# A two-layer hybrid encoder trunk on one core: the token sublayer resequenced, and eight of 22 up tiles as seven half-size products

## The chip, the cores and the metric

The kernel runs on one core of a Trainium2 chip, written by hand in a tile framework: the program names tiles and engines, the framework adds the semaphores and, where the program does not fix an order, plans the order of each engine's instructions by its own costs. The engines are PE (TensorE, matmuls and transposes), DVE (VectorE), ACT (ScalarE), POOL (GpSimd) and SP (SyncE, which only issues DMAs here). POOL issues DMAs too, among them all that add to what lies in the destination. The metric is the device time of one execution in microseconds (us).

## The reference

Two layers on x of 512 tokens by 1024 channels, all float32. Each layer has a token sublayer (attention over a 2-D neighbourhood with 8 heads, bidirectional retention with 4 heads, two sigmoid gates, an output projection, LayerNorm) and a channel sublayer (a gated MLP with a depthwise convolution over three tokens, a gated per-layer embedding, LayerNorm).

```python
for i in range(DEPTH):
    proj = x @ w_in[i]
    q_na, k_na, v_na, q_r, k_r, v_r, g_r, gate_a, gate_b = jnp.split(proj, IN_SPLITS, axis=-1)
    ya = neighbourhood_attention(q_na, k_na, v_na, na_rpb[i])      # heads of 64
    yb = bidirectional_retention(q_r, k_r, v_r, g_r, ret_decay_f[i], ret_decay_b[i])
    merged = jax.nn.sigmoid(gate_a) * (ya @ w_branch_a[i]) + jax.nn.sigmoid(gate_b) * (yb @ w_branch_b[i])
    y = merged @ w_out[i]
    x = layer_norm(DEEPNORM_ALPHA * x + y, ln1_g[i], ln1_b[i])
    ffn = conv_glu_ffn(x, w_up[i], conv_w[i], conv_b[i], w_down[i])   # gelu(conv(x@w_up))[:2816] * [2816:], then w_down
    ple = jax.nn.sigmoid(x @ w_ple_gate[i]) * (p[i] @ w_ple_proj[i])
    x = layer_norm(DEEPNORM_ALPHA * x + ffn + ple, ln2_g[i], ln2_b[i])
```

## The kernel before

**Numbers.** Every operand of a matmul is split in two float32r halves, hi and lo (`split`, L165 and L166: ACT casts hi, DVE subtracts to get lo). A product is three matmuls (`mm3`, L397 to L399): hi·hi, hi·lo, lo·hi. In the stretches of written order a helper records the instructions, and these all have the line L96.

**Weights.** All weights lie packed in DRAM as 148 chunks of 128 x 1024 per layer (512 KB each). `Stream` walks through one long list of items, `seq`, in the order in which the matmuls want them: `fetch` and `load` read a chunk over SP's queue, `prep` splits it, `get` hands it out and looks ahead (`deep` for the splits, `LOOK` for the loads). An item marked `sent` gets its lo from ACT (minus hi) and an accumulating DMA that adds the chunk again, in place of DVE's subtraction.

**Blocks of seven products.** Most projections with a 1024-wide output half are computed as a 2 x 2 block product with seven half-size products instead of eight (`block_items`, `block`): the products are called a, c, t1, t2, d, t3, t4. Their operands are sums of quarters of x (`quad_sums`, made by DVE and split) and sums of weight quarters. A weight sum is made in place, chunk by chunk: t1 adds a chunk to what a used, t2 to that, t4 to that; t3 and d have their own. The addition is an accumulating DMA from POOL's queue (`add`), or, where `ON_CHIP` names the product, a POOL tensor_tensor of two chunks that are on chip. An item named in a HELD list keeps its split halves in the big pool of 30 tiles of 4 KB per partition, and can be prepared early; the others rotate through `N_W` = 3 pairs.

**Token sublayer, per layer.** First `vg`: four blocks of seven products (0 and 1: retention's v and g; 2 and 3: the two gates, stored to DRAM in `g_scr`), in the written order of the list `VG`, with one q and one k tile. Then a phase without written order: the fillers in `FILL` (q and k tiles of retention, `nq` and `nk` tiles and `vn` of the attention), and after them `bb`, the block product of retention's output with w_branch_b. One filler is one slot of the loop; a retention head (`ret_head`, four steps) starts at the slot that `RET_AT` says, an attention head (`na_head`, three steps) at that of `NA_AT`. `na_head` ends its softmax with one POOL tensor_tensor that scales S by 1/sum (L1035). `plain_x` (L1080, L1081) applies the previous layer's g and b to x with two POOL passes per tile, in layer 1. After the loop, the attention's output is multiplied with w_branch_a, merged with the gates (`merge`, L1205 and L1206), transposed (`turn`, L1211), and `proj_ln` does the output projection and LN1; `done1` transposes the result for the channel sublayer.

**Channel sublayer.** All in written order. `pg` is the embedding's gate as a block of seven products with three up tiles between. Then three segments of `SEGS` = 3, 4, 4 pairs of up tiles. An up tile (`up_tile`) is two outputs of 128 channels by 512 tokens, each 24 matmuls of 512 columns (`gemm_t`), followed by the convolution (one ACT pass with the centre tap and bias, two DVE passes for the neighbours, straight from PSUM), gelu on ACT and the product of the two on DVE. `up_step` splits the result, and `s_parts` makes the sums of quarters that the down projection wants; the down projection of a segment is again a, c, t1, t2, d, t3, t4, whose results `into` adds to the residual R. The accumulators w and x4 stay in PSUM over all segments.

Of the kernel before, what the change touches and what calls it, by code (L numbers as in the profile page):

```python
# [32 lines left out]
SENT = ((24, 36),)  # L33
HELD = {3: ("a", "c"), 4: ("c",)}
XT_HELD = (("t3",), ("t3", "t4"))
DEEP = 5

FILL = (('nq0', 'q1', 'nk0', 'k2', 'k1', 'vn', 'q2', 'q3', 'k3', 'nq1', 'nk1', 'nq2', 'nq3', 'nk3', 'nk2'),
 ('k1', 'q1', 'nk0', 'nk2', 'nq0', 'nq1', 'q2', 'q3', 'k2', 'k3', 'vn', 'nk1', 'nq2', 'nk3', 'nq3'))
# [4 lines left out]
RESIDENT = {(l, c) for l in range(DEPTH) for c in range(68, 72)}  # L44
# [3 lines left out]
VG = (('p0', 'p1', '2a', '3a', '3c', '2c', '2t1', '2t2', '3t1', '2d', '3t2', '2t3', '3d', '1a', '3t3', '3t4', '2t4', '0a', '0c', '1c', '0t1', '0d', 'q0',  # L48
  '0t2', '1t1', '0t3', '0t4', 'k0', '1d', '1t2', '1t3', '1t4'),
 ('2a', '2c', '3a', '3c', '3t1', '2t1', '3t2', '2d', '3d', '2t2', '0a', '2t3', '3t3', '0c', '2t4', '1a', 'q0', '0t1', '3t4', '0d', '0t2', '1c', '1t1',  # L50
  '1d', '0t3', '0t4', '1t2', 'k0', '1t3', '1t4'))

XN_AT = 5
M_AT = 4
TABLES_AT = (12, 15)
REST_AT = (1, 3, 5, 8, 10, 12)
PEND_AT = (2, 3)
# [4 lines left out]
PG_DEEP = 5  # L62
RES_DMA = (0, 1)
TR_AT = ("c",)
S_AT = ("up0", "t1", "t2", "up1")
A_DEEP = (4, 5, 5)
# [3 lines left out]
VG_HELD = (('0c', '0t1', '1t1', '1t2', '1t4', '2c', '2d', '2t2', '2t3', '3a', '3d', '3t2', '3t3', '3t4'),  # L70
 ('0t1', '0t2', '0t3', '0t4', '1t2', '1t4', '2a', '2c', '2d', '2t1', '2t2', '2t4', '3c', '3t1', '3t2', '3t3'))
ON_CHIP = ('t3', 't2 t3', 't2 t3', 't2 t3')
BB_HELD = ('a', 't1', 't2')
BB_EARLY = 'c'
# [38 lines left out]
def trunk(tc, wpack, x_nat, x_tr, head, p_tr, rpb, decay, ln_par, ln_col, conv, cos_t, sin_t, dist, xi_d, zd, ident_d, out):  # L113
# [4 lines left out]
    with ExitStack() as es:  # L118
# [49 lines left out]
        class Item:  # L168
# [7 lines left out]
            def __init__(self, kind, src, width, pool=None, plus=None, own=None):  # L176
                self.kind, self.src, self.width, self.pool, self.plus, self.own = kind, src, width, pool, plus, own
                self.raw = self.hl = None
                self.nxt = self.early = self.block = self.other = None

                self.sent = kind == "w" and any(a <= src[1] < b for a, b in SENT)

# [39 lines left out]
        def vg_items(l):  # L222

            by = {}
            for b, c0 in enumerate((0, 12, 52, 36)):
                pos = {(q, j): (l, c0 + 2 * i + j, 0, 1024) for i, q in enumerate("acbd") for j in range(2)}
                for it in block_items(pos, {k[1:]: up for k in VG_HELD[l] if k[0] == str(b)}, VG_EARLY, ON_CHIP[b]):
                    it.block = b
                    by.setdefault(f"{b}{it.kind}", []).append(it)
            return [it for k in VG[l] for it in (by[k] if k in by else plain_items(l, k))]  # L230

        def bb_items(l):
# [3 lines left out]
            for it in block_items(pos, {k: up for k in BB_HELD}, BB_EARLY):  # L236
# [18 lines left out]
        def plain_items(l, f):  # L255
# [6 lines left out]
            elif f[0] == "p":  # L262
                cs = [72 + int(f[1])]
            else:
                cs = [24 + 2 * int(f[2]) + "qk".index(f[1])]
            return [Item("w", (l, c, 0, 1024), 1024) for c in cs]

        class Stream:


            def __init__(self):
                self.seq = []
                for l in range(DEPTH):
# [3 lines left out]
                    for f in FILL[l]:  # L277
                        self.seq += plain_items(l, f)
                    self.seq += bb_items(l)
                    for c in range(60, 72):  # L280
                        plain(c)
                    self.seq += pg_items(l)
                    for s, n in enumerate(SEGS):
                        for c in range(UP0 + 2 * max(tile, PG.count("up")), UP0 + 2 * (tile + 2 * n)):
                            plain(c)
# [9 lines left out]
                self.deep = DEEP  # L295
# [75 lines left out]
            def get(self, ahead=None):  # L371
# [15 lines left out]
                self.load(self.nprep + LOOK)  # L387
# [86 lines left out]
        def proj_ln(lh, nchunk, z, add, g, b, done, follow):  # L474
# [11 lines left out]
            drain(gemm_n(lh, nchunk, [], post=lambda t, ps: half(t, 0, ps), ahead=lambda c: max(2, deep - 2 * (nchunk + n1 - 1 - c))))  # L486
            pss = []
            drain(gemm_n(lh, nchunk, pss, upto=n1, ahead=lambda c: max(2, deep - 2 * (n1 - 1 - c))))
            for t in gemm_n_tok(lh, nchunk, pss, nchunk - 4):
                half(t, 1, pss[t])  # L490
                ln_tile(z[t], st[t], g, b, 2 if t == 3 else 1)
# [155 lines left out]
        for l in range(DEPTH):  # L647
# [156 lines left out]

            def vg(steps, S):

                lh = x_lh(S, xt)
                blocks = [block(lh, vg_emit(0)), block(lh, vg_emit(1)), block(lh, gate(0)), block(lh, gate(1))]
# [192 lines left out]
            def na_head(h):  # L1001
# [32 lines left out]
                s4 = S.rearrange("p (g n) -> p g n", g=4)  # L1034
                nc.gpsimd.tensor_tensor(s4, s4, _ap(rc, 0, [[1, 4], [0, 256]]), ALU.mult)  # L1035
# [35 lines left out]
            def plain_x():  # L1071
# [3 lines left out]
                for t in range(4):  # L1075
# [3 lines left out]
                    if l:  # L1079
                        nc.gpsimd.tensor_tensor(z, z, g, ALU.mult)  # L1080
                        nc.gpsimd.tensor_tensor(z, z, b, ALU.add)  # L1081

            M = []

            def bb():
# [21 lines left out]
                def emit(t, hb, src, sign):  # L1107
                    m = M[t][:, hb * 512:(hb + 1) * 512]
                    nc.vector.scalar_tensor_tensor(m, src, sign, m, op0=ALU.mult, op1=ALU.mult)

                step = block(lambda kind, k, s, i: S[kind][s][:, k, i * P:(i + 1) * P], emit)
                quad("a", 0, 0)
                for n, kind in enumerate(BB):
                    if n == XN_AT:
                        plain_x()
                    if n in (0, M_AT):
# [5 lines left out]
                    if n == 4:  # L1122
                        quad("t4", 1, 1)
                    step(kind)
                    yield

# [32 lines left out]
            ws.deep = DEEP  # L1159
# [14 lines left out]
            def fillers():  # L1174
                F = FILL[l]
                for i, f in enumerate(F):
                    if f == "vn":
                        yield from na_v()
                        continue
                    if F[i + 1:i + 2] == ("vn",):  # L1180
                        column_tiles(0)
                    fill[f[:-1]](int(f[-1]))
                    yield
                yield from bb()
# [10 lines left out]


            mt = {(q, h): [up.tile([P, 4, 256], F32R, tag="u", name=nm("mt")) for _ in range(2)] for h in range(2) for q in range(2)}
            sa = []
            for t in range(4):
                sa.append(unit_f("sa"))  # L1200
                nc.sync.dma_start(sa[t], gscr[0][t * P:(t + 1) * P, :])

            def merge(hb, t, ps):
                c = slice(hb * 512, (hb + 1) * 512)
                nc.vector.tensor_mul(sa[t][:, c], ps, sa[t][:, c])  # L1205
                nc.vector.tensor_add(sa[t][:, c], sa[t][:, c], M[t][:, c])  # L1206

            def turn(hb, t):
                ps = bank("tr")
                for k in range(4):  # L1210
                    nc.tensor.transpose(ps[:, k * P:(k + 1) * P], sa[t][:, (4 * hb + k) * P:(4 * hb + k + 1) * P], ident)  # L1211
                ts = slice((t % 2) * P, (t % 2 + 1) * P)
                hi, lo = mt[hb, t // 2]
                split(hi[:, :, ts], lo[:, :, ts], ps.rearrange("p (k c) -> p k c", c=P))

            for hb in range(2):
                pss = []
                for t in gemm_n_tok(lambda k, s, t: yat[k][:, s, t * P:(t + 1) * P], 2, pss, 0):
                    merge(hb, t, pss[t])
                    if hb:  # L1220
                        turn(0, t)
            for t in range(4):
                turn(1, t)
# [34 lines left out]
            _Ordered.on = set(ORD)  # L1258
# [10 lines left out]
            def up_tile(i):  # L1269
                half = []  # L1270
                for ab in range(2):
                    ps = gemm_t(xs)
                    ci = ab * NF + i
# [442 lines left out]
```

## Time and profile before

| | us |
|---|---|
| median of 3 runs | 1759.23 (1758.42 to 1760.92) |
| profiled execution | 1758.02 |
| its span, first to last instruction | 1756.3 |
| mean granted TensorE clock | 0.982 |
| PE busy in the span | 1683.0, 7815 matmuls |
| DVE busy | 1316.5 |
| ACT busy | 945.4 |
| POOL busy | 294.7 |
| moved by DMA | 277.35 MB |

In the trace, layer 0's token sublayer fills the time up to about 482, its channel sublayer that up to about 890; layer 1's token sublayer reaches to about 1362, and its channel sublayer to the end. A group row names line, engine, operation, output <- inputs and shapes, and then total busy time, the mean ns of one, and the engine's idle time ahead of these instructions with what ended it. A matmul's duration counts from its start to its modelled end, so consecutive ones overlap; how fast they follow each other is read from their start times.

### The profile page before, as it was taken

What the parts mean: (1) busy time and instruction counts of PE and PEld (TensorE: products, weight loads), DVE (VectorE), ACT (ScalarE), POOL (GpSimd) and SP (SyncE); (2) the same over time, 40 slices, a digit from 0 to 9 for tenths busy, and PEclk for the clock granted to TensorE, in tenths of its full rate; (3) what the DMA queues carried; (4) which work ended last, traced back from release to release, by engine and by line L of the source; (5) the groups of instructions that cost most, each with busy time, mean ns of one, the idle gap of its engine ahead of it and who ended that gap; (6) DMA issues with size and microseconds to landing.
All of it is one profiled execution on the core that took longest, in us unless ns stands there. A gap on an engine that the chain in (4) does not pass through costs nothing.

```text
span 1756.3 us, 21209 instructions
## 1 busy us (share of the span) xinstructions
PE 1683.0 (96%) x7815; PEld 1395.4 (79%) x7815; DVE 1316.5 (75%) x1908; ACT 945.4 (54%) x1434; POOL 294.7 (17%) x238
## 2 busy tenths in 40 slices
PE   9699999999999999999988999998889999999997
PEld 7587888877888888888876778887668888888886
DVE  5867568898687867667877766867986878676678
ACT  6555576773266545345555655568622665443452
POOL 1504011320110100000142220122421101000003
PEclk9899999999999999999999999999989999999999
DMA  8686455764754535527766745367538546356375
GB/s 284 186 250 171 108 138 127 173 176 152 219 144 133 131 113 164 143 85 204 199 219 175 200 119 132 85 156 187 161 117 255 144 129 136 107 160 141 96 203 96
DMA packets 81896, 277.35 MB, mean 158 GB/s; under 512 B 9473, under 2 KB 9985, under 8 KB 81793
## 3 DMA queue, kind: packets, MB, share of 16 engines
q1 hardware_dynamic: 60768, 201.55, 33.3%
q0 software_dynamic: 21024, 74.46, 24.8%
q8 instruction: 61, 1.00, 0.2%
q14 instruction: 43, 0.34, 0.1%
HBM read 257.10 MB, written 17.83 MB: 157 GB/s over the span
## 4 chain that ended last, share of the span: by engine, by line
PE 79%; DVE 11%; ACT 4%; DMA 3%; issue 2%; SPq 0%; POOL 0%; DVEq 0%; ACTq 0%; POOLq 0%
PE gt L96 28%; PE u L96 15%; PE v L96 7%; PE w L96 4%; PE gn L398 3%; PE gn L399 3%; PE gn L397 3%; PE gt L399 2%; PE gt L397 2%; PE gt L398 2%; DVE lo L166 2%; DVE lo L96 2%; PE x L96 2%; DVE s L96 1%; ACT hi L96 1%
## 5 line engine op out<-in xcount | busy, mean ns | idle before, releaser
L96 PE MATMUL gt<-x1t,hi 128*128 128x512 f32 x1408 | 433.4, 389 | 0.0
L96 PEld LDWEIGHTS gt<-x1t,hi 128*128 128x128 f32 x1408 | 264.3, 188 | 54.7
L96 PE MATMUL gt<-x1t,lo 128*128 128x512 f32 x704 | 274.1, 389 | 0.1
L96 DVE TENSOR_TENSOR lo<-raw,hi 128x1024 fp32r<-128x1024 f32 (+1 forms) x146 | 174.8, 1206 | 48.5 <-ACT hi L96 48.2
L96 DVE TENSOR_TENSOR lo<-rawa,hi 128x1024 fp32r<-128x1024 f32 x122 | 148.4, 1228 | 72.3 <-ACT hi L96 71.9
L96 DVE SCALAR_TENSOR_TENSOR ca<-gt,cw,ca 128x511 f32<-128x511 f32 x176 | 131.8, 749 | 79.1 <-ACT ca L96 76.0
L96 ACT CAST hi<-raw 128x1024 fp32r<-128x1024 f32 (+1 forms) x149 | 153.0, 1037 | 37.8 <-PE u L96 13.5
L96 PEld LDWEIGHTS gt<-x1t,lo 128*128 128x128 f32 x704 | 132.1, 188 | 28.5 <-DVE lo L96 1.0
L96 ACT CAST hi<-rawa 128x1024 fp32r<-128x1024 f32 x122 | 122.9, 1021 | 52.1 <-DMA rawa<-in_wpack 17.5
L96 ACT ACTIVATE ca<-gt,cw 128x512 f32<-128x512 f32 x88 | 68.6, 779 | 131.4 <-PE gt L96 131.4
L96 POOL DMA_DIRECT2D rawa<-in_wpack x80 | 70.0, 900 | 390.8 <-DVE lo L96 336.6
L96 PE MATMUL u<-hi,s 128*128 128x512 f32 x320 | 105.0, 401 | 11.0 <-ACT s L96 9.8
L96 PE MATMUL v<-hi,s 128*128 128x512 f32 x320 | 106.3, 404 | 9.5 <-ACT hi L96 7.7
L399 PE MATMUL gt<-xt,lo 128*128 128x512 f32 x224 | 87.5, 391 | 1.5 <-DMA lo<-in_wpack 0.8
L397 PE MATMUL gt<-xt,hi 128*128 128x512 f32 x224 | 87.9, 393 | 0.0
L398 PE MATMUL gt<-xt,hi 128*128 128x512 f32 x224 | 87.3, 390 | 0.0
L96 PE MATMUL u<-hi,xt 128*128 128x512 f32 x256 | 81.1, 390 | 3.1 <-DVE p L96 3.1
L96 PEld LDWEIGHTS v<-hi,s 128*128 128x128 f32 x320 | 63.0, 197 | 24.8 <-ACT hi L96 9.0
L96 PEld LDWEIGHTS u<-hi,s 128*128 128x128 f32 x320 | 62.2, 195 | 25.1 <-ACT s L96 10.2
L165 ACT CAST hi<-raw 128x1024 fp32r<-128x1024 f32 x41 | 43.1, 1051 | 57.4 <-PE gn L399 26.0
L96 PE MATMUL v<-lo,s 128*128 128x512 f32 x160 | 65.3, 408 | 6.4 <-DVE lo L96 6.4
L166 DVE TENSOR_TENSOR lo<-raw,hi 128x1024 fp32r<-128x1024 f32 x41 | 50.7, 1237 | 26.6 <-ACT hi L165 26.3
(366 smaller groups left out, 3932.3 us busy)
## 6 DMA issues: line engine op xcount, KB each, us to landing
raw<-in_wpack SPq DMA_DIRECT2D x207, 512.0 KB, 4.1
rawa<-in_wpack POOLq DMA_DIRECT2D x90, 512.0 KB, 5.9
rawa<-in_wpack SPq DMA_DIRECT2D x34, 512.0 KB, 6.4
rawt<-in_wpack SPq DMA_DIRECT2D x34, 512.0 KB, 7.1
lo<-in_wpack POOLq DMA_DIRECT2D x24, 512.0 KB, 5.9
rawt<-in_wpack POOLq DMA_DIRECT2D x18, 512.0 KB, 6.6
rawd<-in_wpack SPq DMA_DIRECT2D x16, 512.0 KB, 9.6
r_scr<-pp SPq DMA_DIRECT2D x8, 512.0 KB, 12.1
```

The costliest lines, as they stand in the source:

```text
L96: r = f(*a, **k)
L165: nc.scalar.copy(hi, src)
L166: nc.vector.tensor_sub(lo, src, _f(hi))
L397: nc.tensor.matmul(ps, lh, rh, start=start, stop=False, skip_group_check=more)
L398: nc.tensor.matmul(ps, lh, rl, start=False, stop=False, skip_group_check=more)
L399: nc.tensor.matmul(ps, ll, rh, start=False, stop=stop, skip_group_check=more)
```

## The change

The four gate and v/g blocks are no longer a phase of their own. `VG` keeps only the first nine or eleven keys in written order; the rest of the blocks' products stand in `FILL`, in the phase without written order, between the attention's tiles, with the retention's q and k tiles behind them. Attention heads start early (slots 6 to 23), retention heads late (31 to 39). The product with w_branch_a becomes the last filler (`ba`), the merge is done in pieces there and in `bb`, and the transposes (`turn`) follow one step of `bb` later. Nearly all weight sums that POOL made on chip become accumulating DMAs (`ON_CHIP` keeps one product of layer 0: two chunks). The softmax scaling moves from POOL to ACT (heads in `RC_ACT`) or DVE, in four pieces; the two passes of `plain_x` move from POOL to DVE. 7 weight chunks instead of 24 are `sent`.

```diff
-SENT = ((24, 36),)
+SENT = (('k3', 'q2'), ('k2', 'k3', 'nk2', 'nq3', 'q1'))
-FILL = (('nq0', 'q1', 'nk0', 'k2', 'k1', 'vn', 'q2', 'q3', 'k3', 'nq1', 'nk1', 'nq2', 'nq3', 'nk3', 'nk2'),
...
+FILL = (('2c', '3t2', '3d', 'nk1', 'vn', '3t3', '3t4', '2t1', 'nk2', '2t2', '2d', '2t3', '0a', 'nq2', 'k2', '0t1', '2t4', '0t2', '0d', '0t3', '1a', 'q0',
+  'k0', '0t4', '1t1', '0c', 'k1', 'q1', '1t2', '1d', 'k3', 'q3', '1t3', '1c', 'q2', '1t4', 'ba'),
...
-RET_AT = ((5, 6, 13, 14), (3, 5, 11, 11))
-NA_AT = ((6, 11, 14, 16, 18, 19, 19, 19), (10, 13, 16, 16, 16, 19, 19, 19))
+RET_AT = ((33, 32, 38, 37), (31, 38, 36, 39))
+NA_AT = ((10, 13, 13, 16, 18, 19, 20, 23), (6, 9, 9, 10, 11, 11, 17, 20))
...
+VG = (('p0', 'p1', '3a', 'nq0', 'nk3', 'nq3', '3c', '3t1', 'nk0', '2a', 'nq1'), ('3a', '2a', '2c', '3c', '3t1', 'nq0', 'nk1', 'nk0', '3t2'))
...
-ON_CHIP = ('t3', 't2 t3', 't2 t3', 't2 t3')
+ON_CHIP = (('', '', 't2', ''), ('', '', '', ''))
+RC_ACT = ((0, 2, 3, 5, 6, 7), (3, 4, 6))
...
-                nc.gpsimd.tensor_tensor(s4, s4, _ap(rc, 0, [[1, 4], [0, 256]]), ALU.mult)
+                for g in range(4):
+                    if h in RC_ACT[l]:
+                        nc.scalar.activation(S[:, g * 256:(g + 1) * 256], S[:, g * 256:(g + 1) * 256], AF.Copy, scale=rc[:, g:g + 1])
+                    else:
+                        nc.vector.tensor_scalar_mul(S[:, g * 256:(g + 1) * 256], S[:, g * 256:(g + 1) * 256], rc[:, g:g + 1])
...
-                        nc.gpsimd.tensor_tensor(z, z, g, ALU.mult)
-                        nc.gpsimd.tensor_tensor(z, z, b, ALU.add)
+                        nc.vector.tensor_mul(z, z, g)
+                        nc.vector.tensor_add(z, z, b)
...
+                    nc.vector.tensor_add(sa[t][:, c], sa[t][:, c], m)
+                    turns.append((hb, t))
```

In the channel sublayer, the last four up tiles of segments 1 and 2 become one block of seven products (`up_block`): 1024 channels of output by 512 tokens, transposed, so that the weights stay the stationary operand and half of the tokens (256 columns) stream. The sums of x that this needs are those of the embedding's gate (`SX`); each is stored to DRAM when it is made (`s_store`, on POOL's queue) and loaded again in segments 1 and 2 (`s_load`). The products' results are put together in `h` tiles on chip (ACT copies, DVE additions), and the convolution then reads those instead of PSUM. It is cut into pieces called chores (`lin` for the linear side, `gates` for the other, then two `s_parts`), which are called a few at a time between the next matmuls by the counts in `CHORES`, or when the down projection wants a pair that is not ready. Segments 1 and 2 are no longer in written order. The accumulator x4 is taken afresh in each segment and added into R.

```diff
+UB = ((), ('up', 'up', 'a', 'c', 'up', 't1', 't2', 'd', 't3', 't4', 'up'), ('a', 'up', 'c', 't1', 'up', 't2', 'd', 't3', 't4', 'up', 'up'))
+UB_HELD = (('t1', 't2', 't3', 't4'), ('a', 'd', 't2', 't3', 't4'), ('c', 't2', 't3', 't4'))
+MLP_DEEP = 4
+SEG_ORD = ((1, 0), (0, 0), (0, 0))
+CHORES = ((4, 4, 4), (4, 1, 3), (4, 0, 7))
+S_LOAD_AT = (0, 0, 3)
...
+                def product(kind, ps, first):
...
+                    for j in range(2):
+                        hi, lo = ws.get()
+                        chore(CHORES[s][1])
+                        for c in range(4):
+                            o = ps[c // 2][:, (c % 2) * 256:(c % 2 + 1) * 256]
+                            for kk in range(2):
+                                k, w = 2 * j + kk, slice(kk * 512 + c * P, kk * 512 + (c + 1) * P)
+                                mm3(o, hi[:, w], lo[:, w], r(k, 0), r(k, 1), first and k == 0 and c % 2 == 0, k == 3 and c % 2 == 1, True)
...
+                        chores.extend((lambda i=i, a=a: lin(i, a)) for a in range(2) for i in range(2))
...
+                        chores.extend(gates())
+                        chores.extend([lambda: s_parts(*sums.pop(0))] * 2)
...
+            def s_store(i):
+                kind = ("t1", "t2", "d", "t3")[i]
+                for j in range(2):
+                    nc.gpsimd.dma_start(sscr[2 * i + j], flat(SX[kind][j]))
...
+                if UB[s]:
+                    step, j = up_block(s), 0
+                    ws.deep = UB_DEEP[s]
+                    for i, kind in enumerate(UB[s]):
+                        if i == S_LOAD_AT[s]:
+                            s_load()
+                        if kind == "up":
+                            up_step(j, False, CHORES[s][0])
+                            j += 1
+                        else:
+                            step(kind)
...
-                    product("t4", x4, s == 0)
+                    product("t4", x4, True)
+                    for i in range(2):
+                        into(2 + i, N1, x4[i])
```

Beside these, the lists of held and early items, the look-ahead counts and the slots of smaller steps have new values, and the first half of `proj_ln` walks token tile by token tile.

More of the change, by code (lines that the diff above doesn't have):

```diff
@@ L65 @@
 S_AT = ("up0", "t1", "t2", "up1")
-A_DEEP = (4, 5, 5)
+A_DEEP = (4, 4, 3)
 BOUND = ("p0", "t4a", "tr", "t4b", "p1")
@@ L263, in plain_items @@
                 cs = [72 + int(f[1])]
+            elif f == "ba":
+                cs = range(60, 64)
             else:
                 cs = [24 + 2 * int(f[2]) + "qk".index(f[1])]
-            return [Item("w", (l, c, 0, 1024), 1024) for c in cs]
+            its = [Item("w", (l, c, 0, 1024), 1024) for c in cs]
+            for it in its:
+                it.sent = f in SENT[l]
+            return its
         class Stream:
@@ L485, in proj_ln @@
             deep = 4 + follow
-            drain(gemm_n(lh, nchunk, [], post=lambda t, ps: half(t, 0, ps), ahead=lambda c: max(2, deep - 2 * (nchunk + n1 - 1 - c))))
+            pss = []
+            for t in gemm_n_tok(lh, nchunk, pss, 0):
+                half(t, 0, pss[t])
             pss = []
@@ L1527, in trunk @@
                 if s == 0:
-                    w, x4 = two("w"), two("x4")
+                    w = two("w")
+                x4 = two("x4")
                 ws.deep = A_DEEP[s]
                 product("a", u, True)
-                ws.deep = DEEP
-                s_parts(*sums.pop())
+                ws.deep = MLP_DEEP
+                if not UB[s]:
+                    s_parts(*sums.pop())
                 if fin and not last:
@@ L1641, in _pack @@
     su = _stat(w_up)
+    blocks = [2 * sum(SEGS[:s + 1]) - 4 for s in range(3) if UB[s]]
     for i in range(NF):
-        ch += [su[i], su[NF + i]]
+        if i in blocks:
+            ch += list(_mov(np.concatenate([w_up[:, i * P:(i + 4) * P], w_up[:, DFF + i * P:DFF + (i + 4) * P]], axis=1)).reshape(-1, P, 1024))
+        if not any(b <= i < b + 4 for b in blocks):
+            ch += [su[i], su[NF + i]]
     ch += _blocks(w_down)
```

310 lines of the change are left out of this document (230 added, 80 removed), and 2 rows, old and new, of the table FILL.

## The prediction

> **What bounds the kernel now.** I read the page first, then busy time by stretch, then PE's waits, then single groups. Times are microseconds, the last figures of a group row are busy time and mean ns of one.
>
> ```profile
> span 1756.3 us, 21209 instructions
> PE 1683.0 (96%) x7815; PEld 1395.4 (79%) x7815; DVE 1316.5 (75%) x1908; ACT 945.4 (54%) x1434; POOL 294.7 (17%) x238
> PE 79%; DVE 11%; ACT 4%; DMA 3%; issue 2%; SPq 0%; POOL 0%; DVEq 0%; ACTq 0%; POOLq 0%
> ```
>
> PE carries the chain for 79%. Its "96% busy" flatters it, because matmul durations overlap. The chain in order of time gives the true spacing:
>
> ```profile
> 615.01 87.04 PE gt L96 x384
> 702.05 5.44 PE u L96 x24
> ```
>
> 384 matmuls of 512 columns take 87.04, so one takes 0.2267 (the group rows give it 389 ns). With that unit I count how full PE is in each stretch (columns: stretch, length, then PE, PEld, DVE, ACT, POOL busy with instruction counts, granted clock, DMA share, GB/s):
>
> ```profile
> 0.00:75.00 75.00, 59.62 (x240) 45.77 (x240) 48.97 (x53) 42.64 (x61) 22.98 (x18) 0.91 0.77 245
> ...
> 350.00:450.00 100.00, 94.99 (x473) 78.26 (x471) 84.42 (x142) 53.87 (x103) 10.63 (x7) 0.98 0.61 180
> ...
> 615.00:740.00 125.00, 125.00 (x554) 103.48 (x553) 87.12 (x115) 54.90 (x71) 6.93 (x8) 1.00 0.50 137
> 740.00:865.00 125.00, 125.00 (x553) 103.37 (x552) 94.88 (x130) 56.01 (x74) 9.24 (x10) 1.00 0.53 151
> 865.00:937.00 72.00, 61.86 (x264) 49.35 (x263) 59.55 (x57) 44.28 (x70) 28.27 (x16) 0.93 0.71 214
> 937.00:1075.00 138.00, 132.25 (x569) 107.48 (x570) 88.26 (x88) 76.49 (x99) 27.41 (x19) 0.99 0.57 158
> ...
> 1175.00:1225.00 50.00, 45.24 (x262) 39.37 (x261) 36.08 (x91) 32.67 (x69) 14.47 (x14) 0.93 0.72 171
> 1225.00:1275.00 50.00, 41.09 (x212) 34.03 (x210) 47.86 (x76) 31.25 (x65) 22.32 (x12) 0.95 0.56 164
> 1275.00:1320.00 45.00, 38.96 (x170) 31.66 (x171) 37.09 (x45) 12.95 (x18) 8.65 (x3) 0.90 0.39 134
> ```
>
> In the channel sublayer (615 to 865) PE has no hole: 554 x 0.2267 = 125.6 of 125. There only less PE work helps. The holes are in the token sublayer. Start: 240 x 0.2267 = 54.4 of 75, 20.6 lost. Layer 1's start (865 to 937): 264 x 0.2267 = 59.8 of 72, 12.2 lost. 937 to 1075: 129.0 of 138, 9.0 lost. 350 to 450: 5.0 idle, and 7 with the clock of 0.98. Layer 1's end (1175 to 1320): 4.8 + 8.9 + 6.0 = 19.7 idle, up to 30 if the clock lost (0.93, 0.95, 0.90) is added in full; I use 26. Together some 75.
>
> Who is late in these holes:
>
> ```profile
> PE u L96 <- ACT s L96: 9.8, 1, 9.8
> PE u L397 <- DVE p L708: 8.5, 1, 8.5
> PE v L96 <- ACT hi L96: 7.7, 3, 4.4
> PE v L96 <- DVE lo L96: 6.4, 5, 3.2
> ```
>
> Weight splits, operand sums and the merge: DVE, with ACT ahead of it. And DVE is slow there for a reason that the groups show:
>
> ```profile
> L96 POOL TENSOR_TENSOR rawt<-rawt,rawd 128x1024 f32<-128x1024 f32 x16 | 43.5, 2754 | 31.4 <-DMA rawt<-in_wpack 31.4
> L96 POOL TENSOR_TENSOR rawa<-rawa,rawd 128x1024 f32<-128x1024 f32 x12 | 34.7, 2894 | 43.7 <-DMA rawd<-in_wpack 31.0 <-DVE lo L96 7.1 <-PE v L96 5.7
> L1035 POOL TENSOR_TENSOR S<-S,rc 128x1024 f32<-128x1024 f32 x16 | 31.0, 1935 | 49.5 <-DVE rc L1033 47.5 <-PE w L399 2.0
> L1080 POOL TENSOR_TENSOR xn<-xn,lng 128x1024 f32<-128x1024 f32 x4 | 11.4, 2862 | 15.2 <-PE v L399 15.2
> ...
> L96 DVE TENSOR_TENSOR s<-xf,xf 128x512 f32<-128x512 f32 x8 | 14.2, 1815 | 0.0
> L96 DVE TENSOR_TENSOR s<-xf 128x512 f32<-128x512 f32 x8 | 5.1, 685 | 0.0
> ```
> ```profile
> 927.94 6.00 DVE L96 TENSOR_TENSOR s<-xf,xf 128x512 f32<-128x512 f32 x2
> ```
> ```profile
> 927.78 5.00 POOL L96 TENSOR_TENSOR rawt<-rawt,rawd 128x1024 f32<-128x1024 f32 x2
> ```
>
> The same subtraction takes 685 ns or, beside a POOL addition, 1815. At 927.9 two of them take 6.00 (two free ones: 1.37) exactly while POOL adds two weight chunks for 5.00.
>
> **The change: PE work.** Per block four up tiles (192 matmuls of 512 columns, 192 x 0.2267 = 43.5) become seven products of 48 matmuls of 256 columns. Their price stands in the retention heads, where 36 run without a gap:
>
> ```profile
> 255.75 0.28 PE L397 MATMUL o<-vh,a 128*128 128x256 f32 x1
> ...
> 259.94 0.28 PE L399 MATMUL o<-su,qx 128*128 128x256 f32 x1
> ```
>
> (259.94 - 255.75) / 35 = 0.120, not half of 0.2267. So 336 x 0.120 = 40.3, and a block saves 3.2, not the 5.4 of an eighth. Four blocks: **-12.8**, bounds -12.8 to -10 (0.122 beside other work).
>
> The Trainium skill (TensorE: Matmul & The Clock Gate, LDWEIGHTS and Back-to-back issue gap) puts a load of 128 weight columns at 107 ns and a matmul of 256 columns at 109. By those figures a block would be an estimated 36.6 and four would save 27 instead of 12.8. The same page's goal table asks for dimensions of at least 512 for good efficiency, which speaks against the narrow products; the row agrees with that direction.
>
> **The change: what the blocks cost DVE, ACT and DMA.**
>
> ```profile
> L96 DVE TENSOR_TENSOR lo<-raw,hi 128x1024 fp32r<-128x1024 f32 x142 | 172.0, 1220 | 46.5 <-ACT hi L96 46.2
> L96 DVE SCALAR_TENSOR_TENSOR ca<-gt,cw,ca 128x511 f32<-128x511 f32 x176 | 131.8, 749 | 79.1 <-ACT ca L96 76.0
> L96 DVE TENSOR_TENSOR R<-R,u 128x512 f32<-128x512 f32 x48 | 30.3, 680 | 0.0
> L96 DVE TENSOR_TENSOR sa<-ta,sa 128x512 fp32r<-128x512 f32 x22 | 15.2, 692 | 15.2 <-ACT sa L96 15.2
> L96 DVE TENSOR_TENSOR ta<-ca,ca 128x256 f32<-128x256 f32 x22 | 9.2, 418 | 0.0
> ...
> L940 DVE TENSOR_SCALAR yb<-yb,rstd 128x256 f32<-128x256 f32 x32 | 10.0, 350 | 5.4 <-POOL rstd L447 5.4
> ```
> ```profile
> L96 ACT CAST hi<-raw 128x1024 fp32r<-128x1024 f32 x145 | 150.5, 1048 | 34.5 <-PE x L96 11.3 <-PE u L96 10.3 <-DMA raw<-in_wpack 6.2
> L96 ACT COPY p<-u 128x512 f32<-128x512 f32 x20 | 11.8, 595 | 13.5 <-PE u L96 13.4
> ```
>
> 14 weight chunks are split instead of 8: DVE +6 x 1.22 = 7.3, ACT +6 x 1.05. Evacuation adds six DVE adds (4.1) and eight ACT copies (4.8); the fresh x4 adds two DVE adds (1.4). So DVE goes from 87.1 and 94.9 of 125 to about 100 and 108 of 122: 82% and 88%, still under PE. ACT goes to 66 and 67. The danger is the end of the block, where work bunches. After t3, DVE owes the convolutions of eight tiles (8 x 2 x 0.749 = 12.0), four gate products (2.8), the splits (2.2) and two s_parts (2 x (4 x 0.418 + 2 x 0.692) = 6.1): 23.1. The down product "a" needs its first 14 of them. PE's cover in segment 1 is t4 (48 x 0.120 = 5.8), one up tile (48 x 0.2267 = 10.9) and the first half of "a" (2.7), 19.4, and DVE owes some 13 there for that tile and the next splits. That is 27 against 19.4: up to 8 late; segment 2 has one tile more. Splits done early into held buffers take part of it. I take 2.25 a block, **+9**; bounds 0 and 32 (8 x 4).
>
> ```profile
> q1 hardware_dynamic: 60768, 201.55, 33.3%
> q0 software_dynamic: 21024, 74.46, 24.8%
> ...
> rawa<-in_wpack POOLq DMA_DIRECT2D x90, 512.0 KB, 5.9
> ```
>
> Queue time per MB is 0.333 x 1756 / 201.55 = 2.90 on SP's queue and 5.85 on POOL's, which so far accumulates. A block adds eight accumulating chunks (4.2 MB x 5.85 = 24.5) and eight loads of stored sums on POOL's queue (4.2 MB at 2.90 to 5.85, 12 to 24.5). Segment 1's DMA share goes from 0.50 to (62.5 + 37 to 49) / 122 = 0.81 to 0.91. That fits, without much room. The eight stores per layer stand in POOL's order between the gate's accumulations, 0.9 of issue each; nothing but the next accumulations is behind them, so nothing is added.
>
> **The change: the token sublayer.** 26 of the 28 weight sums leave POOL for accumulating DMAs; the softmax scaling and the two LN passes over xn leave POOL for ACT and DVE; the gate blocks stand beside the attention, and the merge and its transposes stand inside the last retention block. Each hole by itself:
> - Start: behind four block products come q/k tiles, which want one split per 5.44 of PE where a block product wants two, and no summed weights. Of the waits of 9.8 and 4.4 I take **-8**, bounds 0 and -14.
> - 350 to 450, DVE-bound: attention starts earlier and is spread: **-4**, bounds 0 and -7.
> - Layer 1's start: DVE lost 4.6 at 927.9 alone. Without POOL's additions, and with three tiles ahead of the t2s: **-9**, bounds 0 and -12. What is late next are the accumulations, 5.9 to land where POOL took 2.75.
> - 937 to 1075: **-3**, bounds 0 and -9.
> - Layer 1's end: DVE 47.9 of 50 beside xn's passes on POOL, several heads in one slot. Spread heads, a merge in pieces: **-19**, bounds 0 and -30.
> - Against it: DVE takes xn (8 x 1.22), the seven heads not given to ACT (28 x 0.350) and 17 fewer weights are finished by DMA (17 x 1.22): 40 more on DVE, less what it no longer loses to POOL (9.0 in the s group alone). Hidden where PE is dense, exposed where it isn't: **+6**, bounds 0 and +20.
>
> The Trainium skill (SBUF — State Buffer, Who interferes with whom) has GpSimd and a two-input DVE operation hold one shared port by turns, each for its whole instruction; by that rule the removal of POOL's passes is a full gain, and the 6.00 beside 5.00 above agrees.
>
> Sum: -12.8 + 9 - 8 - 4 - 9 - 3 - 19 + 6 = -40.8. The profiled execution took 1758.0 (span 1756.3 and 1.7 around it), which gives 1717.2. The median 1759.23 lies 1.2 higher: **1718**.
>
> **Rivals.**
> 1. DMA crowds the blocks. From the loads to t4, DMA has 55 to 67 of work (eight fetches 12.2, eight accumulations 24.5, two up tiles 6, loads 12 to 24.5) against PE's 62.1. At the upper end each block waits 5: +20, **1738**. For it: shares of 0.77 already go with holes at the start. Against: the average fits.
> 2. Slower: the block's end is exposed. If the planner puts the 23.1 of DVE after t4, all of it stands before the down products: 4 x (23.1 - 2.25) = 83, **1801**. It decides from (1759 + 3.5 - 1718) / 4 + 2.25 = 13 a block. Against: half of the chain (lin) can start at t3.
> 3. The token sublayer gains nothing: written order is off in the fused part, and each sum lands 3.1 later than POOL finished it, so that one late weight replaces the other. The -43 and the +6 fall away: 1718 + 37 = **1755**, with some 5 either way.
> 4. Narrow matmuls run at the skill's 109 ns (the row says 120): 1718 - 14 = **1704**.
>
> **Chances.** Forecast 0.62 (its own range 1696 to 1735), rival 1 0.15, rival 2 0.08, rival 3 0.12, rival 4 0.03. A measurement of this kernel tells 0.2% (3.5) from nothing. Faster: 0.62 + 0.15 + 0.03 + half of rival 3 = 0.86. Same: a quarter of rival 3, 0.03. Slower: 0.08 + 0.03 = 0.11. The range 1694 to 1748 holds the forecast and rivals 1 and 4, about 0.8.
>
> **What would show it.** 7815 - 768 + 1344 = 8391 matmuls; narrow up matmuls 0.120 apart; no POOL tensor_tensor over 1000 columns outside the last LN and two chunk sums; the s group near 685; segments 1 and 2 near 122 with PE still full; a granted clock nearer 1.00 in the token stretches. Wrong: PE waits at the first down product above 13 a block, or the holes at layer 1's ends as wide as before.

## The result, and the profile after

| | us |
|---|---|
| before, median of 4 runs | 1759.35 (1758.42 to 1760.92) |
| changed kernel, median of 4 runs | 1688.48 (1686.92 to 1689.77) |
| ratio, 95% interval | 0.9596 (0.9579 to 0.9613) |
| span of the profiled execution | 1687.3 |

The change saves 70.9 us, 4.0%. The forecast was 1718 with a range from 1694 to 1748: the direction was right, the size was not, and the time lies 5.5 below the range.

The page of the changed kernel, first lines, chain and DMA queues:

```profile
span 1687.3 us, 22720 instructions
PE 1656.4 (98%) x8391; PEld 1399.0 (83%) x8391; DVE 1314.1 (78%) x2019; ACT 996.3 (59%) x1520; POOL 232.2 (14%) x277
...
q0 software_dynamic: 33840, 121.13, 36.7%
q1 hardware_dynamic: 60768, 201.55, 33.0%
...
PE 59%; DVE 14%; issue 13%; DMA 8%; ACT 3%; POOL 1%; SPq 0%; DVEq 0%; POOLq 0%; ACTq 0%
```

DVE works as long as before (1314.1 against 1316.5) in a span that is 69 shorter, and POOL's queue moves 47 MB more. The share of PE in the chain falls from 79% to 59%, although PE is fuller than before: where several engines are busy nearly all the time, the chain can change hands more often (a reading, not tested). In any case this share does not measure how much PE bounds the kernel. The stretches do (columns: stretch, length, PE, PEld, DVE, ACT, POOL busy with counts, granted clock, DMA share, GB/s):

```profile
0.00:75.00 75.00, 68.42 (x285) 52.80 (x286) 50.71 (x83) 47.66 (x73) 6.94 (x13) 1.00 0.84 258
75.00:200.00 125.00, 124.89 (x599) 103.28 (x597) 80.35 (x132) 95.95 (x167) 16.97 (x16) 1.00 0.73 197
200.00:350.00 150.00, 149.27 (x803) 127.71 (x802) 124.22 (x238) 97.37 (x174) 16.34 (x19) 1.00 0.56 151
350.00:450.00 100.00, 95.95 (x458) 79.41 (x457) 79.08 (x116) 42.50 (x57) 11.96 (x14) 0.98 0.69 197
581.00:703.00 122.00, 121.28 (x688) 105.69 (x687) 94.82 (x130) 66.40 (x88) 19.10 (x25) 1.00 0.79 217
703.00:824.00 121.00, 120.62 (x690) 106.40 (x690) 97.41 (x134) 65.55 (x86) 18.20 (x24) 1.00 0.75 201
824.00:900.00 76.00, 76.00 (x354) 63.41 (x353) 61.90 (x86) 48.98 (x76) 13.12 (x14) 1.00 0.92 266
900.00:1025.00 125.00, 124.90 (x622) 105.23 (x621) 82.89 (x162) 99.85 (x191) 12.18 (x14) 1.00 0.67 174
...
1225.00:1300.00 75.00, 70.14 (x330) 57.44 (x329) 65.50 (x87) 25.23 (x42) 9.41 (x8) 1.00 0.73 237
```

The start has 285 matmuls in 75 us where it had 240: 285 x 0.2267 = 64.6, so 10.4 are lost instead of 20.6. From 75 to 350 PE is full. At the layers' ends (350 to 450, and up to 1300) a few us remain. The stretches from 581 to 824, where the two segments with blocks lie in layer 0, run at PE 121.3 of 122 and 120.6 of 121, with DMA's share at 0.75 to 0.79. Segment 1 itself begins at 595.97; in 596 to 718 and 718 to 840 DVE is busy for 95.7 and 96.6 of 122, ACT for 65.3 and 64.9, and DMA's share is 0.78 and 0.75.

Layer 1's start (824 to 1025 holds it now) has no hole left. Before, 9.0 were lost in 937 to 1075, and more than the 12.2 of the prediction's count in 865 to 937: 32 of its 264 matmuls there are transposes of 128 columns, which follow one another in 0.109 (16 in 1.75 us, first row below). So 232 x 0.2267 + 32 x 0.109 = 56.1 of 72, and 15.9 were lost. A hole that the prediction does not list lay in 75 to 200 before (second row): 519 matmuls of 512 columns take 117.7 of 125, so 7.3 were lost.

```profile
868.06 1.75 PE tr L96 x16
...
75.00:200.00 125.00, 120.28 (x519) 98.05 (x519) 89.55 (x104) 75.33 (x97) 32.87 (x21) 0.98 0.67 180
```

The longest waits of PE are now short, and the sums of x are no longer slow beside POOL. The waits (total, times, longest), then the group:

```profile
PE gt L109 <- DVE lo L109: 2.2, 1, 2.2
PE tr L1134 <- DVE sa L1179: 2.2, 2, 1.6
PE u L435 <- DVE lo L179: 2.0, 1, 2.0
```
```profile
L109 DVE TENSOR_TENSOR s<-xf,xf 128x512 f32<-128x512 f32 x6 | 3.9, 688 | 0.0
```

And the narrow matmuls of the first block's product a, first and last of its 48 in the timeline:

```profile
617.73 0.28 PE L434 MATMUL u<-x1t,hi 128*128 128x256 f32 x1
...
623.37 0.28 PE L436 MATMUL u<-x1t,lo 128*128 128x256 f32 x1
```

(623.37 - 617.73) / 47 = 0.120, as the retention heads showed.

Two landmarks split the gain by stage: the first product R x gate of the embedding, which stands near the beginning of each channel sublayer, and the first transposes of the residual at the end of layer 0's channel sublayer (868.06 above, and 845.62 here).

```profile
498.30 1.29 DVE L96 TENSOR_TENSOR R<-R,psg 128x512 f32<-128x512 f32 x2
...
1378.24 1.29 DVE L96 TENSOR_TENSOR R<-R,psg 128x512 f32<-128x512 f32 x2
```
```profile
479.09 1.29 DVE L109 TENSOR_TENSOR R<-R,psg 128x512 f32<-128x512 f32 x2
...
1313.60 1.29 DVE L109 TENSOR_TENSOR R<-R,psg 128x512 f32<-128x512 f32 x2
```
```profile
845.62 1.75 PE tr L1740 x16
```

The first pair is of the kernel before, the others of the changed one. Layer 0's token sublayer, up to 498.30 and 479.09, saved 19.2. Its channel sublayer, from there to the transposes, went from 369.8 to 366.5: 3.2. From the transposes to the second product, 510.2 became 468.0, so layer 1's token sublayer saved 42.2. Behind that, to the end of the span, 378.1 became 373.7: 4.4. The two token sublayers together saved 61.4 of the 69.0, the two channel sublayers 7.6.

### The profile page after: what moved, and what is told of

It is laid out like the page before. It is cut to its first block, busy times and chain, and to the rows that moved or that the text cites. A ratio compares the mean times of both kernels' runs of the same rounds, so it can differ in the third digit from the quotient of the medians.

```text
span 1687.3 us, 22720 instructions
## 1 busy us (share of the span) xinstructions
PE 1656.4 (98%) x8391; PEld 1399.0 (83%) x8391; DVE 1314.1 (78%) x2019; ACT 996.3 (59%) x1520; POOL 232.2 (14%) x277
## 4 chain that ended last, share of the span: by engine, by line
PE 59%; DVE 14%; issue 13%; DMA 8%; ACT 3%; POOL 1%; SPq 0%; DVEq 0%; POOLq 0%; ACTq 0%
PE u L435 4%; PE u L436 4%; PE u L434 4%; DMA rawa<-in_wpack 4%; PE gt L434 4%; PE gt L435 4%; PE gt L436 4%; PE gt L109 3%; DVE lo L179 3%; PE gn L436 3%; PE gn L434 3%; PE gn L435 3%; PE v L434 3%; PE v L436 3%; PE v L435 3%
## 5 line engine op out<-in xcount | busy, mean ns | idle before, releaser
L179 DVE TENSOR_TENSOR lo<-raw,hi 128x1024 fp32r<-128x1024 f32 (+1 forms) x156 | 188.9, 1217 | 97.6 <-ACT hi L178 97.0
L179 DVE TENSOR_TENSOR lo<-rawa,hi 128x1024 fp32r<-128x1024 f32 (+1 forms) x151 | 180.3, 1201 | 64.0 <-ACT hi L178 63.0
L178 ACT CAST hi<-rawa 128x1024 fp32r<-128x1024 f32 (+1 forms) x151 | 154.4, 1032 | 125.9 <-DMA rawa<-in_wpack 49.7
L109 PE MATMUL gt<-x1t,hi 128*128 128x512 f32 x384 | 118.3, 389 | 0.0
L434 PE MATMUL gt<-x1t,hi 128*128 128x512 f32 x256 | 99.7, 390 | 0.0
L435 PE MATMUL gt<-x1t,hi 128*128 128x512 f32 x256 | 99.7, 390 | 0.0
L436 PE MATMUL gt<-x1t,lo 128*128 128x512 f32 x256 | 99.6, 389 | 0.0
L109 PEld LDWEIGHTS gt<-x1t,hi 128*128 128x128 f32 x384 | 72.1, 188 | 15.0
L109 PE MATMUL gt<-x1t,lo 128*128 128x512 f32 x192 | 74.9, 390 | 0.1
L109 DVE TENSOR_TENSOR lo<-raw,hi 128x1024 fp32r<-128x1024 f32 (+1 forms) x46 | 54.5, 1197 | 5.2 <-ACT hi L109 4.9
L436 PEld LDWEIGHTS gt<-x1t,lo 128*128 128x128 f32 x256 | 48.1, 188 | 10.1
L434 PEld LDWEIGHTS gt<-x1t,hi 128*128 128x128 f32 x256 | 48.1, 188 | 9.6
L435 PEld LDWEIGHTS gt<-x1t,hi 128*128 128x128 f32 x256 | 48.1, 188 | 9.5
L179 DVE TENSOR_TENSOR lo<-rawt,hi 128x1024 fp32r<-128x1024 f32 (+1 forms) x36 | 42.8, 1193 | 14.8 <-ACT hi L178 14.6
L436 PE MATMUL gn<-hi,mt 128*128 128x512 f32 x128 | 49.3, 391 | 1.5 <-DVE mt L179 1.5
L435 PE MATMUL u<-lo,s 128*128 128x512 f32 x128 | 50.4, 394 | 0.0
```

Of the source, the lines that this page charges most:

```text
L109: r = f(*a, **k)
L178: nc.scalar.copy(hi, src)
L179: nc.vector.tensor_sub(lo, src, _f(hi))
L434: nc.tensor.matmul(ps, lh, rh, start=start, stop=False, skip_group_check=more)
L435: nc.tensor.matmul(ps, lh, rl, start=False, stop=False, skip_group_check=more)
L436: nc.tensor.matmul(ps, ll, rh, start=False, stop=stop, skip_group_check=more)
```

## The experiments

Times are medians of four to ten runs, except where another number is given. The kernel before took 1758.5 to 1760.0 beside them.

**1. The parts by themselves.** First the blocks, taken out of the changed kernel:

```diff
-UB = ((), ('up', 'up', 'a', 'c', 'up', 't1', 't2', 'd', 't3', 't4', 'up'), ('a', 'up', 'c', 't1', 'up', 't2', 'd', 't3', 't4', 'up', 'up'))
+UB = ((), (), ())
```

> The changed kernel with its eight up tiles per layer computed as plain up tiles again (no blocks, no stored sums). The channel sublayer of layer 1 got 4.4 us shorter, which for two layers makes 8.8: this run should take about 1697 us (0.3 to 0.7% more than the changed kernel). The prediction's own figures (12.8 of PE work less 9 of stalls) say 1692. If the blocks were worth nothing or cost time, 1688 or less. A rival, that the stored sums and accumulations crowd DMA, says less than 1685.

1694.84, ratio 0.9635 (0.9616 to 0.9653). The blocks are worth 6.4: half of the 12.8 of PE work. The landmarks say 7.6, which is within what the two intervals allow.

Then POOL's passes, put back into the changed kernel, and on the other side taken out of the kernel before, whose order stays:

```diff
 changed kernel:
-ON_CHIP = (('', '', 't2', ''), ('', '', '', ''))
+ON_CHIP = (('t3', 't2 t3', 't2 t3', 't2 t3'), ('t3', 't2 t3', 't2 t3', 't2 t3'))
 and the softmax scaling (L1076 and on) and the two passes over xn as nc.gpsimd.tensor_tensor again
 kernel before:
-ON_CHIP = ('t3', 't2 t3', 't2 t3', 't2 t3')
+ON_CHIP = ('', '', '', '')
 and the softmax scaling on ACT (heads of RC_ACT) or DVE, xn on DVE
```

> The changed kernel with all POOL passes back: 28 weight sums on chip, the softmax scaling and the two passes over xn. Theory A (these passes hold up DVE, and their removal is most of the 60 us that the token sublayers gained): 1718 to 1730 us. Theory B (the new order gained it, and spreads DVE's work so far that POOL's passes are hidden): under 1700 us.

> The kernel before with no POOL pass left but those of the last LN: all weight sums by DMA, softmax scaling on ACT and DVE, xn on DVE, in the old order. Theory A: 1720 to 1732 us. Theory B: 1750 us or more, since the holes of the old order stay.

1707.53 (ratio 0.9703, 0.9686 to 0.9721) and 1744.21 (0.9915, 0.9900 to 0.9931). Both times lie between the two theories, outside the range of either. Theory A falls, and B in its strong form too: the passes are worth 19 in the new order and 15 in the old one. What is left between the old order without POOL's passes (1744.2) and the changed kernel without blocks (1694.8), 49.4, is the order with what belongs to it: slots of the heads, the merge in pieces, held lists, look-ahead counts, and fewer chunks finished by DMA (experiment 5). With POOL's passes in both kernels it comes to 45 (1759.1 to 1707.5, less the 6.4 of the blocks). This is what is left over, not the effect of one part. The kernel before without the passes shows why freeing DVE is not enough: its page and two of its stretches

```profile
PE 1677.9 (96%) x7815; PEld 1393.0 (80%) x7815; DVE 1267.2 (73%) x1944; ACT 959.3 (55%) x1470; POOL 188.7 (11%) x214
```
```profile
1200.00:1250.00 50.00, 39.98 (x209) 33.57 (x210) 44.73 (x92) 38.61 (x83) 3.48 (x4) 0.90 0.56 143
1250.00:1300.00 50.00, 42.25 (x188) 33.70 (x187) 42.86 (x56) 17.78 (x26) 0.00 (x0) 0.93 0.38 140
```

say that DVE has 49 less to do in all, and is still at 86% to 89% from 1200 to 1300, where PE idles 10.0 and 7.8. The work of that stretch is bunched; that it goes a little faster does not move it elsewhere.

Two runs split POOL's passes:

> The changed kernel with only the 28 weight sums back on POOL (softmax scaling and xn stay off it). All POOL passes together cost 19 us in this order. If the sums carry it (their holes lie in the first 100 us): 1700 us or more. If the softmax scaling and xn carry it: 1693 us or less.

> The changed kernel with only the softmax scaling and the two passes over xn back on POOL. If the weight sums carry the 19 us: 1690 to 1695 us. If these passes carry it: 1700 us or more. The prediction's own term for moving them to ACT and DVE was a cost of up to 20 us, by which this run would be the faster one: under 1685 us.

The weight sums alone on POOL give 1717.99 (0.9769, 0.9741 to 0.9796), the softmax scaling and xn alone 1692.56 (0.9619, 0.9603 to 0.9635). So the sums carry it. Moving the other two off POOL did not cost time; the 4 that it seems to save are within the two intervals. That the sums alone cost more (29.5) than all passes together (19.0) means that the parts don't add up: the token phase has no written order, so the planner lays it out anew for each kernel. Why it comes out that way was not settled, and a few us of any difference between two orders of the token phase may be this. The start of the run with the sums alone, to be read against 93.42 of 100 in the changed kernel's first 100 us:

```profile
0.00:100.00 100.00, 88.87 (x354) 68.84 (x355) 69.02 (x96) 61.62 (x93) 17.48 (x16) 0.95 0.72 229
200.00:275.00 75.00, 66.51 (x319) 54.43 (x318) 56.01 (x97) 56.76 (x108) 10.53 (x6) 0.95 0.34 96
```

354 matmuls against 393 at the start, and a new hole at 200 to 275.

**2. Where the attention heads stand.** In the changed kernel:

```diff
-NA_AT = ((10, 13, 13, 16, 18, 19, 20, 23), (6, 9, 9, 10, 11, 11, 17, 20))
+NA_AT = ((13, 13, 13, 19, 19, 19, 23, 23), (9, 9, 9, 11, 11, 11, 20, 20))
```

> The changed kernel with attention heads put three and two to a slot (as before the change) instead of nearly one each. If spreading the heads fills the holes: 1698 us or more. If where the heads stand among the fillers matters little: 1686 to 1692 us.

1738.87 (0.9885, 0.9865 to 0.9905): 50 of the 71 us are gone. Some heads also start up to three slots later here; nothing else is changed. Three of its stretches and five of its longest waits:

```profile
150.00:175.00 25.00, 19.59 (x86) 15.48 (x85) 15.29 (x31) 21.31 (x42) 1.74 (x2) 0.86 0.55 147
250.00:285.00 35.00, 23.38 (x91) 18.42 (x90) 23.62 (x33) 15.89 (x25) 2.59 (x3) 0.76 0.41 108
1060.00:1085.00 25.00, 19.44 (x82) 15.81 (x81) 10.26 (x27) 14.58 (x31) 2.60 (x3) 0.86 0.69 178
```
```profile
PE v L434 <- ACT p L737: 5.6, 1, 5.6
PE pt L1089 <- DVE t L881: 4.1, 1, 4.1
PE gt L434 <- DVE pt L179: 3.9, 1, 3.9
PE u L434 <- DVE pt L179: 3.6, 1, 3.6
PE v L434 <- DVE pt L179: 3.2, 1, 3.2
```

No engine is full in the first two holes (DVE 15 and 24 of 25 and 35, ACT 21 and 16), nor in the third (10 and 15 of 25). Three of the five waits, 10.7 in all, are for the splits of a head's transposed exponentials (`pt`), and the changed kernel's list has no such wait. That fits a chain: a head's scores, exponentials, scaling, transposes and splits each wait for another engine, and PE waits in its order for one of them. The granted clock in these stretches is 0.76 to 0.86. The longest wait, for `p`, is for a result of a gate block. That three heads at once give PE three such chains and too few products between is the reading that fits these rows; the run does not separate it from the later slots. The same in the old order without POOL's passes, layer 1 alone:

```diff
-NA_AT = (..., (10, 13, 16, 16, 16, 19, 19, 19))
+NA_AT = (..., (9, 11, 15, 16, 17, 18, 18, 19))
```

> The old order with no POOL pass (1744.2 us), and layer 1's attention heads spread as evenly as the old list of fillers allows (slots 9, 11, 15, 16, 17, 18, 18, 19 instead of 10, 13, 16, 16, 16, 19, 19, 19). If bunching by slot alone makes the hole of 26 us at layer 1's end: 1725 to 1735 us. If it is that the whole attention stands behind the gate blocks, in too few slots: 1740 us or more.

1737.48 (0.9873, 0.9856 to 0.9890): 6.7 better, between the two expectations. Spreading helps, but in the old list several of the q/k tiles stand as late as slots 14 to 17, a head can't start before its own, and the gate blocks are done before the first slot. In the new list the gate blocks stand beside the heads. That this is what gives spreading its worth was not tested by itself.

**3. The first products.** Layer 0, then layer 1, in the changed kernel:

```diff
-VG = (('p0', 'p1', '3a', 'nq0', 'nk3', 'nq3', '3c', '3t1', 'nk0', '2a', 'nq1'),
+VG = (('p0', 'p1', '3a', '3c', '2a', '3t1', 'nq0', 'nk3', 'nq3', 'nk0', 'nq1'),
...
- ('3a', '2a', '2c', '3c', '3t1', 'nq0', 'nk1', 'nk0', '3t2'))
+ ('3a', '2a', '2c', '3c', '3t1', '3t2', '3d', 'nq0', 'nk0'))
```

(The second with nk1 in the later place of 3d.)

> The changed kernel with layer 0's first products in another order: the four block products 3a, 3c, 2a, 3t1 ahead of the five q/k tiles of the attention, instead of these between them. If the q/k tiles fill the start's hole because they want one weight split per 5.44 us of PE: 1694 to 1700 us (6 to 11 back). If the absence of chip sums is enough: 1687 to 1690 us.

> The changed kernel with layer 1's first products in another order: after 3t1 the products 3t2 and 3d come ahead of the attention's q/k tiles. If the tiles between fill the hole at layer 1's start (16 us in the kernel before, 7 with POOL's passes off and the old order, none after): 1692 to 1696 us. If the absence of POOL's sums is enough: 1687 to 1690 us.

1697.76 (0.9651, 0.9637 to 0.9666) and 1691.94 (0.9619, 0.9597 to 0.9641). The q/k tiles are worth 9.3 at the start:

```profile
0.00:75.00 75.00, 66.43 (x256) 50.85 (x257) 46.89 (x78) 43.18 (x67) 6.63 (x12) 0.91 0.80 257
```

256 matmuls instead of 285, though no weight sum is on POOL in these products. In layer 1 the order brings back a hole,

```profile
875.00:900.00 25.00, 21.18 (x83) 16.21 (x82) 15.23 (x21) 12.54 (x19) 4.38 (x5) 0.93 0.95 248
```

83 x 0.2267 = 18.8 of 25, 6.2 lost. The total is 3.5 above the changed kernel's, but the two intervals overlap, so that it does not show a loss.

**4. The end of a block.** In the changed kernel no piece of a block's convolutions is handed out ahead of need:

```diff
-CHORES = ((4, 4, 4), (4, 1, 3), (4, 0, 7))
+CHORES = ((4, 4, 4), (0, 0, 0), (0, 0, 0))
```

> The changed kernel with no chore handed out ahead of need in segments 1 and 2: each piece of a block's convolutions and gates is written only where the down projection wants the pair. If the 23 us of DVE work behind each block are really hidden by being spread among PE's products, this exposes 10 to 20 us of them per block: 1728 to 1768 us. If the planner orders them freely whatever the place in the program: 1687 to 1692 us.

1759.18 (ratio to before 1.0004, 0.9992 to 1.0016): 70.7 more, 17.7 per block. The whole gain of the change is gone.

```profile
PE u L434 <- ACT a L178: 39.5, 4, 11.4
PE v L434 <- ACT sa L178: 7.2, 6, 2.4
```
```profile
PE 1675.1 (95%) x8391; PEld 1409.4 (80%) x8391; DVE 1319.5 (75%) x2019; ACT 996.4 (57%) x1520; POOL 229.9 (13%) x277
```
```profile
675.00:700.00 25.00, 14.26 (x53) 10.35 (x52) 22.45 (x35) 15.57 (x24) 0.86 (x1) 0.80 0.13 22
```

Four waits of about 10, one per block, for the first operand of the down projection, with DVE at 22.45 of 25 and the clock at 0.80 in the stretch. This is rival 2's mechanism at its place; the counts in CHORES avoid it. The span is 71.5 longer (1758.8): 52.8 of that is more idle time of PE, and 18.7 is more busy time for the same 8391 matmuls, at a mean granted clock of 0.979 instead of 0.997.

**5. Weights finished by DMA.** 21 instead of 7 in the changed kernel, then none; and none instead of 24 in the kernel before, with POOL's passes and without:

```diff
 changed kernel:
-SENT = (('k3', 'q2'), ('k2', 'k3', 'nk2', 'nq3', 'q1'))
+SENT = (('k3', 'q2', 'nq2', 'nk1', 'nk2', 'vn'), ('k2', 'k3', 'nk2', 'nq3', 'q1', 'nk3', 'nq1', 'nq2', 'vn'))
 and, in another run, SENT = ((), ())
 kernel before:
-SENT = ((24, 36),)
+SENT = ()
```

> The changed kernel with 21 instead of 7 of the attention's and retention's weight chunks finished by DMA in place of DVE's subtraction (17 us less on DVE, as in the kernel before for these tiles). If DVE's total work still sets the holes that are left in the token sublayers: 1680 to 1686 us. If what is left are waits in order of arrival, or DMA and POOL's queue: 1687 to 1695 us.

> The changed kernel with no weight chunk finished by DMA: all 7 that still are go to DVE's subtraction. If each such chunk costs in this order (21 cost 40 us more than 7): 1680 to 1687 us. If the 7 left stand where they are free or help: 1688 to 1700 us.

> The kernel before with none of its 24 weight chunks finished by DMA (29 us more of work on DVE, POOL's passes stay). If fewer such chunks are a gain by themselves, whatever the order: 1735 to 1750 us. If they paid in the old order, where DVE is slowed by POOL's passes: 1762 us or more.

> The old order with no POOL pass (1744.2 us) and no chunk finished by DMA. What is left to the changed kernel without blocks (1694.8 us) is then order, and slots of smaller steps. If the chunks cost time by themselves: 1725 to 1738 us, order 30 to 43. If not: 1742 us or more, order near 50.

1728.58 (0.9824, 0.9805 to 0.9844) with 21; 1686.54 (0.9585, 0.9572 to 0.9598) with none, which the interval does not tell from the changed kernel's; 1760.43 (1.0002, 0.9993 to 1.0011) and 1750.37 (0.9944, 0.9931 to 0.9958) in the old order. With 18 us less work on DVE (1295.8 busy), the first of these is 40 slower, which neither expectation allowed. Its longest wait of PE shows where:

```profile
PE gt L436 <- DMA lo<-in_wpack: 19.4, 3, 9.6
```
```profile
84.54 0.86 POOL L394 DMA_DIRECT2D lo<-in_wpack  x1 [0.50 <-ACT lo L393]
...
99.27 0.79 PE L436 MATMUL gt<-xt,lo 128*128 128x512 f32 x1 [9.62 <-DMA lo<-in_wpack]
```

PE waits three times for the accumulating DMA itself. Its idle time in the whole run is 57.9 (1727.3 less 1669.4 busy) against 30.9 in the changed kernel, 27.0 more, and 19.4 of that are these waits. The longest ends 14.7 us after POOL issued an accumulation at 84.54, which it did 0.3 after ACT had written minus hi; the other two end 8.8 and 8.7 after the issue. DVE's subtraction, which the DMA replaces, takes 1.22. So a chunk finished by DMA comes that much later, and here PE has reached it first. Why the first took 14.7 is open: the DMA engines are full in 84 to 100 (share 1.06), but so they are in the changed kernel's same stretch (1.01). In the old order the 24 chunks were neither gain nor loss (the time lies between the two expectations), or a gain of 6 where POOL's passes are off, where the two intervals just touch. So this part of the change explains none of the 49.

## Why the prediction was right and wrong

**Right: the price of a narrow matmul.** 0.120, and 8391 matmuls in the trace. Rival 4, the 109 ns worked out from the Trainium skill (TensorE: Matmul & The Clock Gate, Back-to-back issue gap), did not come.

**Right in the main: DVE, ACT and DMA in the segments.** Forecast for DVE about 100 and 108 of 122, measured 95.7 and 96.6; ACT 66 and 67, measured 65.3 and 64.9; DMA share 0.81 to 0.91 in segment 1, measured 0.78. Rival 1 did not come: no wait of PE for a DMA stands in the changed kernel's list. The stalls that the blocks add were put at 9, which leaves 3.8 of the 12.8; without blocks the kernel is 6.4 slower. The term is within its bounds, and a little too large.

**Right in mechanism: rival 2.** 23.1 of DVE work behind each block was priced at 20.9 if exposed; exposed, it cost 17.7.

**Wrong: the sizes of the token sublayer's terms.** This is the step that failed. The sum gave the two token sublayers 37 (43 less 6). The landmarks say 61.4, and without the blocks the changed kernel is 64.3 faster than before (1759.1 to 1694.8). By terms:

| term | forecast | measured |
|---|---|---|
| start, to 75 | -8, at most -14 | -10.2 (20.6 to 10.4 lost) |
| 75 to 200 | no term | -7.3, no hole left |
| 350 to 450 | -4, at most -7 | about -1 (5.0 to 4.1 idle) |
| layer 1's start | -9, at most -12 | -15.9, no hole left |
| 937 to 1075 | -3, at most -9 | -9.0, no hole left |
| layer 1's end | -19, at most -30 | about -17 (42.2 less 24.9) |
| more work on DVE | +6, at most +20 | no cost shown |
| sum | -37 | about -60 |

Four things miss some 28 between them, and the terms for 350 to 450 and for layer 1's end give 5 of that back. First, 75 to 200 stands in no line of the prediction (7.3). Second, the two holes at layer 1's start were put at 12 and were worth 24.9: part of that is the count, which took transposes for matmuls of 512 columns (12.2 for 15.9), and the rest is that each hole got only a share of itself. Third, the +6 for 40 more of DVE work. Runs on both sides of it say that DVE's total is not the price: 25 more on DVE in the old order change nothing (1760.4), 49 less gain 15, and 18 less in the new order lose 40. What these runs fit is that it matters when a result comes, more than how much an engine does in all. Fourth, the start's hole, put 2.2 too small.

The range failed for the same reason. By the prediction's own bounds these terms could fall by 35 more (6, 3, 3, 6, 11 and 6), to 1683, and its lower end allowed 24 of that. Whether the holes fill together, because one new order fills them, or each for a cause of its own, stays open: experiments 2 and 3 undo the heads and the start one at a time.

**Wrong: the weight given to POOL.** The prediction read the slow sums (1815 ns beside POOL, 685 alone) as the reason why DVE is late. The reading of the rows holds: the group is at 688 now. The rule of the Trainium skill (SBUF — State Buffer, Who interferes with whom) agrees with it. But as the cause of the holes it was too much: without the passes DVE's busy time fell by 49 and the time by 15 in the old order, and the passes are worth 19 in the new one, of some 61. Rival 3 (nothing gained, since a DMA sum lands later than POOL's) did not come either.

## What to carry to other kernels

Where PE should be the bound and isn't, count its instructions by stretch with the true spacing and ask what stands beside the hole, not which engine has the most work: the new order as a whole gave 45 to 49 us, and bunching its attention heads again lost 50, while freeing the busiest side engine in the old order gave 15. Work that moves to a DMA lands later than an engine's pass does: 24 chunks finished that way were free in one order, and 14 more cost 40 us in another. A list of holes should cover every stretch and count narrow matmuls at their own price; and where one change may fill several holes, the range should reach to where it fills them all.

## What the runs showed of the hardware that was not expected

A matmul of 256 columns costs 0.120 us, 53% of one of 512 (0.2267), in streams where every matmul has its own weight load; seven half-size products for eight save 3.2 of 43.5 that way instead of 5.4, before any stall. That price was read from the trace before the change, and it held. And stalls of PE cost more than they last: in the run without early chores PE is idle for 52.8 us more, and the same 8391 matmuls are busy for 18.7 more, at a mean granted clock of 0.979 instead of 0.997. With the heads bunched the two figures are 33.1 and 16.7 (0.986), with 21 chunks finished by DMA 27.0 and 13.0 (0.989). A small part of that is counting: a matmul of 512 columns is booked for 0.389 and the next one starts 0.2267 later, so each wait shows some 0.16 of busy time that a full stream hides.
